# A mixture-of-experts stage: the seventeenth tile on the last place's weights, and gathers issued later

## The chip, the cores and the metric

The program runs on one core of a Trainium2 chip. The metric is the device time of one execution in microseconds (us), lower is better; of several runs the median counts. The engines are TensorE (PE, matrix products; its weight loads are shown as PEld), VectorE (DVE), ScalarE (ACT), GpSimd (POOL) and SyncE (SP), which here issues the plain DMAs. Gathers through a list of row numbers are issued by POOL. Each engine works through its instructions in the order in which the program gives them.

## The reference, cut to what matters

The reference computes four blocks of mixers on 512 tokens of width 1024, then a second network that ends with a mixture of experts. Only this last stage is touched. All of it is float32.

```python
def _moe(u, router_w, router_bias, w_gate, w_up, w_down):
    t = u.reshape(B * T, D)                              # 512 tokens x 1024
    s = jax.nn.sigmoid((t @ router_w).astype(jnp.float32))
    sb = s + router_bias.astype(jnp.float32)
    # the best of 4 groups of experts, and in it the best 2 of 4 experts
    ...
    combine = ...                                        # 512 x 16, two weights a token
    y = jnp.zeros_like(t)
    for e in range(16):
        h = jax.nn.silu(t @ w_gate[e]) * (t @ w_up[e])   # 1024 -> 512
        y = y + combine[:, e:e + 1] * (h @ w_down[e])    # 512 -> 1024
    return y
```

So each token uses two experts of 16, and how many tokens an expert gets is known only when the program runs: 1024 in all.

## The kernel before, in words

**Tiles.** The stage works on tiles of 128 tokens. Tiles 0 to 15 hold the first 128 tokens of experts 0 to 15. An expert with more tokens needs further tiles. The first of these is tile 16, which the program always computes; its expert's number is read at run time (`e0`, L3650). A loop behind the stage (`For_i`, L3696) would compute any others, one in each pass. `route` (L3374) works out on DVE and PE which tokens go where: `rsel` holds a token's rank among its expert's tokens, `rh` its number and its weight, `posf`/`pos` the row of its result, `ovl` the list of further tiles' experts and their count.

**A tile's work.** `own_hots` compares ranks with 1 to 128 (DVE), and `own` (through `metas`, L3550) multiplies the comparisons with `rh` on PE, which gives for each of the tile's 128 places the row number `ix` and the weight; then a gather (L3560, POOL) fetches these rows of `d_u` into `U[e]`. `turn_u` transposes them on PE and splits the result into a high part (ACT) and a low part (DVE). `up` multiplies with the gate weights (`pg`) and the up weights (`pu`), `gelu` combines the two, `turn_h` transposes again, `down` multiplies with the down weights, ACT scales the result (L3627), and `store` (L3630, SP) writes it to `d_o`. At the end the rows of `d_o` are gathered by `pos` (L3724) and added.

**Weights.** An expert has 12 units of 128 x 1024 numbers (512 KB): 4 gate, 4 up, 4 down. `moe_load` (L3505) issues their loads on SP, through 21 buffers. `split` (L3578) turns the next loaded unit into a high part, cast by ACT (L3582), and a low part, a subtraction (L3583) on POOL for every third unit (j % 3 == 2) and on DVE for the others. There are four buffers for split units. `mm3` (L169) multiplies high by high, high by low (L172 here waits for the weight's low part) and low by high.

**Order.** The order within the stage is written out by hand. For tile e the program goes through `up` for gate, `up` for up and then `down` of tile e - 1, unit by unit, with one `split` behind each unit's matmuls, three units ahead of their use. Of the twelve units that are split in a pass, numbered j modulo 12, gate has 11, 0, 1 and 2, up 3 to 6 and down 7 to 10; POOL's are 11, 2, 5 and 8. Other steps are put between: behind the second up unit (4) come `turn_u(e + 1)` and `own(e + 2)` with its gather, so that the gather stands on POOL ahead of the subtraction of unit 5. In this text "tile 8" as a stretch of time is the pass e = 8, with `down` of tile 7 in it.

Of the kernel before, what the change touches and what calls it, by code (L numbers as in the profile page):

```python
# [97 lines left out]
HLG = ()  # L98
HA = 2
NRAW = 13  # L100
RT_N = 288
NG = 4
PREP_US = 25.68
WG = 1
# [14 lines left out]
class Net:  # L119
# [2682 lines left out]
    def block2(self):  # L2802
        nc, A, v = self.nc, self.A, self.v
        V, S, G, MM = nc.vector, nc.scalar, nc.gpsimd, nc.tensor.matmul
# [486 lines left out]
        d_u = self.dram("d_u", [T, D])  # L3291
        self.raws = []
        units = []
        for e in range(16):
            units += [A["moe_w"][e, j] for j in range(8)] + ([A["moe_w"][e - 1, 8 + j] for j in range(4)] if e else [])
        self.mu = [units, ["wraw"] * 4 + ["whi"] * 2 + ["wlo"] * 2 + ["raw"] * NRAW, 0]
        for _ in range(4):
# [3 lines left out]
        U = {}  # L3301
# [26 lines left out]
        ps = self.psum()  # L3328
# [45 lines left out]
    def route(self, pool):  # L3374

        nc, A = self.nc, self.A
        V, S, G, MM = nc.vector, nc.scalar, nc.gpsimd, nc.tensor.matmul
        TTO = V.tensor_tensor
        lg = self.logits

        def t(name, *shape):
            return pool.tile([P] + list(shape), F32, name="r_" + name)
# [53 lines left out]
        M = []  # L3436
# [36 lines left out]
        V.tensor_copy(rh[:, :, :, 0], tok[:, :, None].to_broadcast([P, 4, 16]))  # L3473
        yield rsel, rh

        lst = t("lst", 8, 16)
        TTO(lst, ovb[:, None, :].to_broadcast([P, 8, 16]), co[:, 24:32, None].to_broadcast([P, 8, 16]), op=OP.is_le)
        oe = t("oe", 8)
        V.tensor_reduce(oe, lst, axis=AX.X, op=OP.add)
        V.tensor_scalar(oe, oe, -1.0, None, op0=OP.add)  # L3480
        V.tensor_reduce(oe[:, 7:8], ov, axis=AX.X, op=OP.add)
        ovl = rp.tile([P, 8], I32, name="ovl")
        V.tensor_copy(ovl, oe)

        r, ge = t("rk", 4, 16), t("ge", 4, 16)
        V.tensor_scalar(r, rsel, -1.0, None, op0=OP.add)
        V.tensor_scalar(ge, r, 127.5, None, op0=OP.is_ge)
        dl = t("dl", 16)
        TTO(dl, ovb, ce, op=OP.subtract)
        V.tensor_scalar(dl, dl, 15.0, 128.0, op0=OP.add, op1=OP.mult)  # L3490
        TTO(ge, ge, dl[:, None, :].to_broadcast([P, 4, 16]), op=OP.mult)
        TTO(r, r, ge, op=OP.add)
        V.scalar_tensor_tensor(r, ce[:, None, :].to_broadcast([P, 4, 16]), 128.0, r, op0=OP.mult, op1=OP.add)
        posf = rp.tile([P, 2, 4], F32, name="posf")
        for k in range(2):
            TTO(M[k], M[k], r, op=OP.mult)
# [3 lines left out]
        src = rp.tile([P, 2, 4, 2], F32, name="src")  # L3500
        V.tensor_copy(src[:, :, :, 0], tok[:, None, :].to_broadcast([P, 2, 4]))
        V.tensor_copy(src[:, :, :, 1], w)
        yield pos, posf, ovl, src

    def moe_load(self):  # L3505

# [15 lines left out]
    def moe(self):  # L3522
# [17 lines left out]
        M, U, UT, HT, TH, O = {}, {}, {}, {}, {}, {}  # L3540

        HOT = {}

# [6 lines left out]
        def metas(e, rhs):  # L3550

            pm = self.psum()
            for i, (o, r) in enumerate(zip(HOT.pop(e), rhs)):
                MM(pm[:, :2], o, r, start=(i == 0), stop=(i == len(rhs) - 1))
            m, ix = tl("meta", (P, 2), 4), tl("ix", (P, 1), 4, I32)
            V.tensor_copy(ix, pm[:, 0:1])
            V.tensor_copy(m, pm[:, 0:2])
            M[e] = m
            U[e] = tl("u", (P, D), 2)
            nc.gpsimd.indirect_dma_start(out=U[e], out_offset=None, in_=d_u,  # L3560
                                         in_offset=bass.IndirectOffsetOnAxis(ap=ix[:, 0:1], axis=0))

        def own_hots(e):
            hots(e, [rsel[:, a, e:e + 1] for a in range(4)], iota)
# [7 lines left out]
        def extra(e):  # L3572
            metas(e, [src[:, k, a, :] for k in range(2) for a in range(4)])
# [21 lines left out]
                self.split(o[:, 0, h:h + 4, :], o[:, 1, h:h + 4, :], p4)  # L3595
            return o

        def up(e, ps):

            for k2 in range(4):  # L3600
                w = W.pop(0)
                for kk in range(2):
                    k = 2 * k2 + kk
                    ws = slice(kk * 512, (kk + 1) * 512)
                    self.mm3(ps, UT[e][:, 0, k, :], UT[e][:, 1, k, :], w[:, 0, ws], w[:, 1, ws], k == 0, k == KC - 1)
# [10 lines left out]
        def down(e):  # L3616
            ps = [self.psum(), self.psum()]
            for k in range(4):
                w = W.pop(0)
                for n in range(2):  # L3620
                    ws = slice(n * 512, (n + 1) * 512)
                    self.mm3(ps[n], HT[e][:, 0, k, :], HT[e][:, 1, k, :], w[:, 0, ws], w[:, 1, ws], k == 0, k == 3)
                split()
                yield
            O[e] = tl("o", (P, D), 2)
            for n in range(2):
                S.activation(O[e][:, n * 512:(n + 1) * 512], ps[n], AF.Copy, scale=M[e][:, 1:2])  # L3627
# [12 lines left out]

        for e in range(2):
            own_hots(e)
            own(e)
        pos, posf, ovl, src = next(route)
# [5 lines left out]
        e0 = nc.values_load(ovl[0:1, 0:1], min_val=0, max_val=15, engines=(mybir.EngineType.SP,))  # L3650

        def unit(e, j):
            return A["moe_w"][bass.ds(e, 1), j].rearrange("o p c -> p (o c)")

        self.mu[0] += [unit(e0, j) for j in range(8)] + [A["moe_w"][15, 8 + j] for j in range(4)]
        self.mu[0] += [unit(e0, 8 + j) for j in range(4)]
        with self.tc.manual_schedule():
            for _ in range(3):
                split()
            turn_u(0)  # L3660
            for e in range(17):
                pg, pu = self.psum(), self.psum()
                for i, _ in enumerate(up(e, pg)):
                    if i == 0 and e:
                        turn_h(e - 1)
                    if i == 2:
                        if e < 14:
                            own_hots(e + 2)
                        elif e == 14:
                            extra_hots(16, base)  # L3670
                for i, _ in enumerate(up(e, pu)):
                    if i == 0 and e > 1:
                        store(e - 2, slot(e - 2))
                    if i == 1 and e < 16:
                        turn_u(e + 1)
                        if e < 14:
                            own(e + 2)
                        elif e == 14:
                            extra(16)
                for i, _ in enumerate(down(e - 1) if e else ()):  # L3680
                    if i == 0:
                        gelu(e, pg, pu)
                if not e:
                    gelu(e, pg, pu)
            turn_h(16)
            store(15, slot(15))
            for _ in down(16):
                pass
            store(16, slot(16))

        g2, lng, lnb = (self.wp.tile([P, UW], F32, name=n, tag="wraw", bufs=4) for n in ("g2", "lng", "lnb"))
        self.row_bcast(g2, self.mods["a4"][:, 40:48, 0])
        nc.sync.dma_start(lng, A["b2_l2g"].partition_broadcast(P))
        nc.sync.dma_start(lnb, A["b2_l2b"].partition_broadcast(P))
        n_ov = nc.values_load(ovl[0:1, 7:8], min_val=0, max_val=7)
        with self.tc.For_i(1, n_ov, 1) as i:  # L3696
            e = nc.values_load(ovl[0:1, bass.ds(i, 1)], min_val=0, max_val=15, engines=(mybir.EngineType.SP,))
# [6 lines left out]
            extra(17)  # L3704
            turn_u(17)
            for _ in range(4):
                split()
            pg, pu = self.psum(), self.psum()
            for ps in (pg, pu):
                for _ in up(17, ps):  # L3710
# [5 lines left out]
            store(17, d_o[bass.ds((i + 16) * P, P), :])  # L3716
        mst.close()

        tst, tp = self.open("tail")
# [74 lines left out]
def host_arrays(I):  # L3794
# [115 lines left out]
    co[:, 32:288] = (np.arange(16)[None] < np.arange(16)[:, None]).reshape(-1)  # L3910
# [27 lines left out]
```

## Time and profile before

| | |
|---|---|
| median of 3 runs | 3840.93 us (3830.1 to 3840.94) |
| the profiled execution | 3836.11 us, its span 3834.3 us |
| PE, DVE, ACT, POOL busy over the span | 87%, 65%, 45%, 35% |
| experts' stage, first matmul to last | 388.13 us, from 3388.87 to 3777.00 |
| loads of expert weights | 204 of 512 KB, 5.2 us from issue to landing |

The page of the profile shows the span in 40 slices of 96 us. The experts' stage fills the last slices but one: the row of DMA shares reads 8 (tenths) there, and the row of TensorE's granted clock, in tenths of 2.4 GHz, 9 in three slices. Groups of instructions by line, waits by line, single tiles and the timeline are asked of the trace separately; times in them are in us from the start of the span.

### The profile page before, as it was taken

What the parts mean: (1) busy time and instruction counts of PE and PEld (TensorE: products, weight loads), DVE (VectorE), ACT (ScalarE), POOL (GpSimd) and SP (SyncE); (2) the same over time, 40 slices, a digit from 0 to 9 for tenths busy, and PEclk for the clock granted to TensorE, in tenths of its full rate; (3) what the DMA queues carried; (4) which work ended last, traced back from release to release, by engine and by line L of the source; (5) the groups of instructions that cost most, each with busy time, mean ns of one, the idle gap of its engine ahead of it and who ended that gap; (6) DMA issues with size and microseconds to landing.
All of it is one profiled execution on the core that took longest, in us unless ns stands there. A gap on an engine that the chain in (4) does not pass through costs nothing. (4 is left out here: it accounts for less than half of the span.)

```text
span 3834.3 us, 63098 instructions
## 1 busy us (share of the span) xinstructions
PE 3337.1 (87%) x24502; PEld 2819.6 (74%) x24502; DVE 2500.9 (65%) x4375; ACT 1713.9 (45%) x2887; POOL 1327.4 (35%) x1559
## 2 busy tenths in 40 slices
PE   4999998988688889989989999899998785778883
PEld 3788887767577787777878887777886675667773
DVE  8777777453576767645445555556666789777767
ACT  4321223433455545645356666532223543346663
POOL 5031002220356767710043332202101556235555
PEclk8999998999788888899999999999998997779997
DMA  5444452246865344463422222345642210288883
GB/s 195 151 146 137 143 198 97 77 162 189 249 181 152 118 142 131 123 216 119 125 73 68 56 67 65 103 151 200 221 148 68 72 55 17 81 297 313 314 310 115
DMA packets 350861, 560.23 MB, mean 146 GB/s; under 512 B 170592, under 2 KB 226016, under 8 KB 350560
## 3 DMA queue, kind: packets, MB, share of 16 engines
q1 hardware_dynamic: 346960, 543.06, 43.7%
q0 software_dynamic: 3600, 13.11, 0.9%
q8 instruction: 194, 3.18, 0.3%
q14 instruction: 107, 0.88, 0.1%
HBM read 457.23 MB, written 88.36 MB: 142 GB/s over the span
## 5 line engine op out<-in xcount | busy, mean ns | idle before, releaser
L162 DVE TENSOR_TENSOR wlo<-wraw,whi 128x1024 fp32r<-128x1024 f32 x220 | 285.8, 1299 | 167.8 <-ACT whi L161 164.5
L171 PE MATMUL ps<-hl,whi 128*128 128x512 f32 (+1 forms) x992 | 363.9, 367 | 1.6 <-ACT hl L1945 1.6
L161 ACT CAST whi<-wraw 128x1024 fp32r<-128x1024 f32 x221 | 231.3, 1047 | 296.6 <-PE ps L172 183.1
L172 PE MATMUL ps<-hl,whi 128*128 128x512 f32 (+1 forms) x992 | 361.3, 364 | 1.5 <-DVE hl L1950 1.5
L173 PE MATMUL ps<-hl,wlo 128*128 128x512 f32 (+1 forms) x992 | 360.4, 363 | 2.5 <-DVE wlo L162 2.5
L3582 ACT CAST e_wsp<-mraw 128x1024 fp32r<-128x1024 f32 x204 | 212.4, 1050 | 105.0 <-issue 52.4
L3583 DVE TENSOR_TENSOR e_wsp<-mraw,e_wsp 128x1024 fp32r<-128x1024 f32 x136 | 187.2, 1399 | 72.9 <-ACT e_wsp L3582 71.6
L3583 POOL TENSOR_TENSOR e_wsp<-mraw,e_wsp 128x1024 fp32r<-128x1024 f32 x68 | 179.8, 2652 | 129.8 <-ACT e_wsp L3582 47.9
L173 PEld LDWEIGHTS ps<-hl,wlo 128*128 128x128 f32 x992 | 188.0, 189 | 34.5 <-DVE wlo L162 3.4
L172 PEld LDWEIGHTS ps<-hl,whi 128*128 128x128 f32 x992 | 187.8, 189 | 34.7 <-DVE hl L1950 4.9
L171 PEld LDWEIGHTS ps<-hl,whi 128*128 128x128 f32 x992 | 187.8, 189 | 32.1 <-ACT hl L1945 2.0
L1522 POOL TENSOR_TENSOR s_tmp<-s_N,s_P 128x15 f32<-128x15 f32 (+4 forms) x360 | 126.4, 351 | 145.4 <-DVE s_N L1506 119.0
L207 DVE SCALAR_TENSOR_TENSOR araw<-araw,conds 128x1024 f32<-128x1024 f32 x128 | 157.6, 1236 | 24.7 <-DMA araw<-ada 24.1
L171 PE MATMUL ps<-whi,hl 128*128 128x512 f32 x320 | 132.5, 414 | 27.3 <-ACT hl L404 25.6
L617 POOL TENSOR_SCALAR v<-v,vr_y 128x256 f32<-128x256 f32 x70 | 93.6, 1355 | 157.8 <-DVE vr_y L270 157.8
L171 PE MATMUL ps<-s,whi 128*128 128x512 f32 (+1 forms) x384 | 138.6, 361 | 0.0
L1523 POOL TENSOR_TENSOR s_P<-s_P,s_tmp 128x15 f32<-128x15 f32 (+4 forms) x360 | 127.5, 354 | 28.2
L172 PE MATMUL ps<-s,whi 128*128 128x512 f32 (+1 forms) x384 | 136.7, 356 | 0.0
L173 PE MATMUL ps<-s,wlo 128*128 128x512 f32 (+1 forms) x384 | 136.5, 356 | 0.2 <-DVE wlo L162 0.2
L172 PE MATMUL ps<-wlo,hl 128*128 128x512 f32 x320 | 132.6, 414 | 4.1 <-DVE wlo L162 3.9
L167 DVE TENSOR_TENSOR a_pt<-ps,a_pt 128x512 fp32r<-128x512 f32 (+1 forms) x128 | 69.3, 554 | 102.2 <-ACT a_pt L166 102.2
L173 PE MATMUL ps<-whi,hl 128*128 128x512 f32 x320 | 131.9, 412 | 1.4 <-DVE hl L411 1.3
(932 smaller groups left out, 10203.7 us busy)
## 6 DMA issues: line engine op xcount, KB each, us to landing
mraw<-moe_w SPq DMA_DIRECT2D x204, 512.0 KB, 5.2
araw<-ada SPq DMA_DIRECT2D x144, 512.0 KB, 3.9
wraw<-sgu_v SPq DMA_DIRECT2D x40, 512.0 KB, 3.6
wraw<-rw_in SPq DMA_DIRECT2D x40, 512.0 KB, 4.8
d_n<-ff SPq DMA_DIRECT2D x48, 384.0 KB, 5.2
s_fn<-d_n SPq DMA_DIRECT2D x24, 768.0 KB, 6.2
wraw<-sgu_out SPq DMA_DIRECT2D x34, 512.0 KB, 4.1
wraw<-sgu_u SPq DMA_DIRECT2D x32, 512.0 KB, 4.6
```

What stands on the lines that cost most here:

```text
L161: self.nc.scalar.copy(hi[:, :cols], t[:, :cols])
L162: (eng or self.nc.vector).tensor_tensor(lo[:, :cols], t[:, :cols], hi[:, :cols], op=OP.subtract)
L167: (eng or self.nc.vector).tensor_tensor(lo, src, hi, op=OP.subtract)
L171: mm(out, lh, rh, start=start, stop=False)
L172: mm(out, lh, rl, start=False, stop=False)
L173: mm(out, ll, rh, start=False, stop=stop)
L207: self.nc.vector.scalar_tensor_tensor(junk, w, 0.5, c, op0=OP.mult, op1=OP.mult, accum_out=out)
L617: e.tensor_scalar(vt[g][:, t, :], vt[g][:, t, :], r[:, t:t + 1], None, op0=OP.mult)
L1522: TTG(o, N[:, None, ts, s].to_broadcast([P, nj, nt]), Pm[:, js, s:s + 1].to_broadcast([P, nj, nt]), op=OP.mult)
L1523: TTG(Pm[:, js, ts], Pm[:, js, ts], o, op=OP.subtract)
L3582: S.copy(hl[:, 0, :], raw)
L3583: (G if j % 3 == 2 else V).tensor_tensor(hl[:, 1, :], raw, hl[:, 0, :], op=OP.subtract)
```

## The change

Experts and tiles are no longer the same numbers. A place (0 to 15) takes the part of the expert's number: the last expert that has more than 128 tokens, if it is not one of the first three (`MFIX`), changes places with expert 15. Tile 16 then belongs to the same expert as tile 15, and the two share each weight unit: `up` and `down` take several tiles, and a pass over tiles 15 and 16 multiplies both with a unit before the next. With that 192 units are loaded and split in place of 204. Where the last such expert is one of the first three, the loop behind the stage starts one tile earlier and computes tile 16 again with that expert's weights (`back`, `es[:, 1:2]`).

Weights of places 3 to 15 are now loaded from an address that SP reads from `ovl` (`placed`). `route` gets the operations that find the expert, exchange the two columns in `rsel` and `rh`, and write the list `il`. The table `low` is turned round (experts behind, not in front).

The gather is taken out of `metas` and becomes a step of its own. For tiles 0 to 2 and for tile 16 it stays where it was in POOL's order. For tiles 3 to 15 it is issued in `down` of the pass, behind the split of the second unit (8). `turn_u(16)` moves from the pass of tile 15 to the end of that of tile 14.

```diff
-RT_N = 288
+RT_N = 304
+MFIX = 3
+MOE_L = 33
@@ block2
-        for e in range(16):
+        for e in range(MFIX):
             units += [A["moe_w"][e, j] for j in range(8)] + ([A["moe_w"][e - 1, 8 + j] for j in range(4)] if e else [])
@@ route
-        lst = t("lst", 8, 16)
-        TTO(lst, ovb[:, None, :].to_broadcast([P, 8, 16]), co[:, 24:32, None].to_broadcast([P, 8, 16]), op=OP.is_le)
-        oe = t("oe", 8)
...
+        rs0 = t("rs0", 4, 16)
+        V.tensor_copy(rs0, rsel)
+        il = t("il", MOE_L)
+        es, no = t("es", 2), t("no", 16)
+        V.tensor_scalar(no, ovb, 0.5, None, op0=OP.is_ge)
+        V.tensor_reduce(es[:, 0:1], no, axis=AX.X, op=OP.add)
+        V.tensor_scalar(es[:, 1:2], es[:, 0:1], MFIX - 0.5, None, op0=OP.is_le)
+        oh, pe = t("oh", 16), il[:, 0:16]
+        V.memset(oh, 0.0)
+        V.tensor_scalar(oh[:, MFIX:], ce[:, MFIX:], es[:, 0:1], None, op0=OP.is_equal)
+
+        TTO(no, co[:, 288:304], oh, op=OP.mult)
+        TTO(pe, ce, no, op=OP.add)
+        V.tensor_reduce(es[:, 0:1], no, axis=AX.X, op=OP.add)
+        TTO(il[:, 15:16], il[:, 15:16], es[:, 0:1], op=OP.subtract)
+        for x in (rsel, rh[:, :, :, 1]):
+            d, ds_ = t("sw", 4, 16), t("sws", 4)
+            TTO(d, x[:, :, 15:16].to_broadcast([P, 4, 16]), x, op=OP.subtract)
+            TTO(d, d, oh[:, None, :].to_broadcast([P, 4, 16]), op=OP.mult)
+            TTO(x, x, d, op=OP.add)
+            V.tensor_reduce(ds_, d, axis=AX.X, op=OP.add)
+            TTO(x[:, :, 15], x[:, :, 15], ds_, op=OP.subtract)
+
+        xi = t("xi", 8)
...
+        ovl = rp.tile([P, MOE_L], I32, name="ovl")
+        V.tensor_copy(ovl, il)
+        back = rp.tile([P, 1], F32, name="back")
+        V.tensor_scalar(back, es[:, 1:2], float(P), None, op0=OP.mult)
@@ metas
-            M[e] = m
+            M[e], IX[e] = m, ix
+
+        def gather(e):
             U[e] = tl("u", (P, D), 2)
...
@@ up, down
-        def up(e, ps):
+        def up(*tiles):
             for k2 in range(4):
                 w = W.pop(0)
-                for kk in range(2):
...
+                for e, ps in tiles:
+                    for kk in range(2):
+                        k = 2 * k2 + kk
+                        ws = slice(kk * 512, (kk + 1) * 512)
+                        self.mm3(ps, UT[e][:, 0, k, :], UT[e][:, 1, k, :], w[:, 0, ws], w[:, 1, ws], k == 0, k == KC - 1)
                 split()
                 yield
@@ the stage
-        self.mu[0] += [unit(e0, j) for j in range(8)] + [A["moe_w"][15, 8 + j] for j in range(4)]
-        self.mu[0] += [unit(e0, 8 + j) for j in range(4)]
+        at = {}
+        def placed(e, j):
+            if e not in at:
+                at[e] = nc.values_load(ovl[0:1, e:e + 1], min_val=MFIX, max_val=15, engines=(mybir.EngineType.SP,))
+            return unit(at[e], j)
+        for e in range(MFIX, 17):
+            self.mu[0] += [lambda e=e, j=j: placed(e, j) for j in range(8 if e < 16 else 0)]
+            self.mu[0] += [A["moe_w"][e - 1, 8 + j] if e == MFIX else lambda e=e, j=j: placed(e - 1, 8 + j) for j in range(4)]
...
-            for e in range(17):
-                pg, pu = self.psum(), self.psum()
-                for i, _ in enumerate(up(e, pg)):
+            for e in range(16):
+                own_e = (e, 16) if e == 15 else (e,)
+                pg, pu = ({t: self.psum() for t in own_e} for _ in range(2))
+                for i, _ in enumerate(up(*pg.items())):
...
-                    if i == 1 and e < 16:
+                    if i == 1 and e < 15:
                         turn_u(e + 1)
                         if e < 14:
                             own(e + 2)
                         elif e == 14:
                             extra(16)
+                            gather(16)
                 for i, _ in enumerate(down(e - 1) if e else ()):
                     if i == 0:
-                        gelu(e, pg, pu)
+                        for t in own_e:
+                            gelu(t, pg[t], pu[t])
+                    if i == 1 and e < 14:
+                        gather(e + 2)
+                    if i == 3 and e == 14:
+                        turn_u(16)
                 if not e:
-                    gelu(e, pg, pu)
-            turn_h(16)
-            store(15, slot(15))
-            for _ in down(16):
+                    gelu(e, pg[e], pu[e])
+                    gather(2)
+            for t in (15, 16):
+                turn_h(t)
+            store(14, slot(14))
+            for _ in down(15, 16):
                 pass
-            store(16, slot(16))
+            for t in (15, 16):
+                store(t, slot(t))
```

## Rows read from the trace of the kernel before

**Rows 1.** Windows: stretch, length; engines' busy us; granted clock, DMA share, GB/s.

```profile
3388.87:3777.00 388.13, 343.04 (x1549) 277.99 (x1549) 283.71 (x313) 258.51 (x301) 203.57 (x82) 0.94 0.84 291
3584.95:3606.92 21.97, 18.94 (x92) 15.55 (x93) 16.50 (x19) 15.38 (x18) 12.23 (x6) 1.00 0.94 343
3606.92:3630.45 23.53, 20.52 (x92) 16.69 (x92) 16.48 (x19) 15.39 (x18) 12.16 (x6) 0.93 0.90 299
3491.00:3494.40 3.40, 3.40 (x9) 2.65 (x9) 0.12 (x1) 1.04 (x1) 2.06 (x1) 0.50 1.03 400
3367.00:3381.00 14.00, 7.05 (x33) 6.97 (x33) 8.52 (x41) 0.17 (x1) 0.46 (x1) 0.50 0.98 393
```

**Rows 2.** The tile mraw: loads, casts, and us from issue to landing.

```profile
L3519 SPq DMA_DIRECT2D mraw<-moe_w x204: 327/328/629, 3281.8 to 3740.0; - x102
...
L3582 ACT CAST e_wsp<-mraw x204: 1027/1052/1069, 3362.0 to 3768.4; 128x1024 fp32r<-128x1024 f32 x102
...
DMA to landing us min/median/max: 3.2/5.2/10.2
```

**Rows 3.** Waits in the stage: total us, times, longest.

```profile
PE ps L172 <- POOL e_wsp L3583: 40.5, 14, 3.0
```

**Rows 4.** Timeline of tile 8: start, us, engine, line, names, [idle before].

```profile
3576.55 0.95 PE L3554 MATMUL ps<-rh,e_hot 128*128 128x2 f32 x8
...
3577.27 1.06 ACT L3582 CAST e_wsp<-mraw 128x1024 fp32r<-128x1024 f32 x1
...
3580.15 2.54 DVE L3583 TENSOR_TENSOR e_wsp<-mraw,e_wsp 128x1024 fp32r<-128x1024 f32 x2
...
3580.34 1.87 POOL L3560 DMA_INDIRECT e_u<-d_u,e_ix  x1 [4.48 <-DVE e_meta L3557]
...
3582.23 5.03 POOL L3583 TENSOR_TENSOR e_wsp<-mraw,e_wsp 128x1024 fp32r<-128x1024 f32 x2
...
3584.95 0.50 PE L172 MATMUL ps<-e_wsp,e_hT 128*128 128x512 f32 x1 [3.02 <-POOL e_wsp L3583]
```

**Rows 5.** Timeline of PE: ends of the waits in tiles 2 and 14.

```profile
3444.21 0.79 PE L172 MATMUL ps<-e_wsp,e_hT 128*128 128x512 f32 x1 [3.03 <-POOL e_wsp L3583]
...
3725.52 0.50 PE L172 MATMUL ps<-e_wsp,e_hT 128*128 128x512 f32 x1 [3.03 <-POOL e_wsp L3583]
```

**Rows 6.** Timeline of PE and POOL in tile 15 and behind it.

```profile
3731.10 0.39 PE L171 MATMUL ps<-e_wsp,e_uT 128*128 128x512 f32 x1
...
3739.76 0.49 PE L3593 MATMUL ps<-ident,e_u 128*128 128x128 f32 x3
...
3746.19 3.26 POOL L3583 TENSOR_TENSOR e_wsp<-mraw,e_wsp 128x1024 fp32r<-128x1024 f32 x1 [1.23 <-issue]
...
3749.03 0.39 PE L171 MATMUL ps<-e_wsp,e_uT 128*128 128x512 f32 x1
...
3751.15 2.80 POOL L3583 TENSOR_TENSOR e_wsp<-mraw,e_wsp 128x1024 fp32r<-128x1024 f32 x1 [1.70 <-ACT e_wsp L3582]
```

**Rows 7.** The tile e_u (gathers): durations, first and last start; us to landing.

```profile
L3560 POOL DMA_INDIRECT e_u<-d_u,e_ix x15: 958/1760/1960, 3401.8 to 3720.8; - x15
...
DMA to landing us min/median/max: 4.9/8.2/8.7
```

**Rows 8.** Timeline of DVE where the stage begins.

```profile
3386.03 0.17 DVE L3499 CAST pos<-posf 128x8 int32<-128x8 f32 x1
...
3388.85 0.69 DVE L167 TENSOR_TENSOR e_uT<-ps,e_uT 128x512 fp32r<-128x512 f32 x1 [2.65 <-ACT e_uT L166]
```

**Rows 9.** The tile e_o (stores): us from issue to landing, shortest, median, longest.

```profile
DMA to landing us min/median/max: 2.6/6.6/7.0
```

**Rows 10.** Timeline of DVE, POOL and PE in tile 1.

```profile
3417.56 7.37 DVE L3583 TENSOR_TENSOR e_wsp<-mraw,e_wsp 128x1024 fp32r<-128x1024 f32 x2 [0.64 <-ACT e_wsp L3582]
...
3418.11 5.73 POOL L3583 TENSOR_TENSOR e_wsp<-mraw,e_wsp 128x1024 fp32r<-128x1024 f32 x2
...
3424.98 0.50 PE L172 MATMUL ps<-e_wsp,e_hT 128*128 128x512 f32 x1 [1.40 <-DVE e_wsp L3583]
```

More of the change, by code (lines that the diff above doesn't have):

```diff
@@ L3474, in route @@
         yield rsel, rh
-        lst = t("lst", 8, 16)
-        TTO(lst, ovb[:, None, :].to_broadcast([P, 8, 16]), co[:, 24:32, None].to_broadcast([P, 8, 16]), op=OP.is_le)
-        oe = t("oe", 8)
[L3479 to L3483, printed above, removed]
+        rs0 = t("rs0", 4, 16)
+        V.tensor_copy(rs0, rsel)
@@ new lines, in route @@
+        xi = t("xi", 8)
+        V.tensor_scalar(xi, co[:, 24:32], es[:, 1:2], None, op0=OP.subtract)
+        lst = m16[:, :8]
+        TTO(lst, ovb[:, None, :].to_broadcast([P, 8, 16]), xi[:, :, None].to_broadcast([P, 8, 16]), op=OP.is_gt)
+        V.tensor_reduce(il[:, 16:24], lst, axis=AX.X, op=OP.add)
+        V.tensor_scalar(il[:, 16:24], il[:, 16:24], 15.0, None, op0=OP.min)
+        V.tensor_scalar(il[:, 24:32], xi, 16.0, None, op0=OP.add)
+        V.tensor_reduce(il[:, 32:33], ov, axis=AX.X, op=OP.add)
@@ L3485, in route @@
+        TTO(il[:, 32:33], il[:, 32:33], es[:, 1:2], op=OP.add)
+        ovl = rp.tile([P, MOE_L], I32, name="ovl")
+        V.tensor_copy(ovl, il)
+        back = rp.tile([P, 1], F32, name="back")
+        V.tensor_scalar(back, es[:, 1:2], float(P), None, op0=OP.mult)
         r, ge = t("rk", 4, 16), t("ge", 4, 16)
-        V.tensor_scalar(r, rsel, -1.0, None, op0=OP.add)
+        V.tensor_scalar(r, rs0, -1.0, None, op0=OP.add)
         V.tensor_scalar(ge, r, 127.5, None, op0=OP.is_ge)
         dl = t("dl", 16)
-        TTO(dl, ovb, ce, op=OP.subtract)
+        TTO(dl, ovb, pe, op=OP.subtract)
@@ L3492, in route @@
         TTO(r, r, ge, op=OP.add)
-        V.scalar_tensor_tensor(r, ce[:, None, :].to_broadcast([P, 4, 16]), 128.0, r, op0=OP.mult, op1=OP.add)
+        V.scalar_tensor_tensor(r, pe[:, None, :].to_broadcast([P, 4, 16]), 128.0, r, op0=OP.mult, op1=OP.add)
         posf = rp.tile([P, 2, 4], F32, name="posf")
@@ L3502, in route @@
         V.tensor_copy(src[:, :, :, 1], w)
-        yield pos, posf, ovl, src
+        yield pos, posf, ovl, src, back
     def moe_load(self):
@@ L3539, in moe @@
         nc.sync.dma_start(iota, A["rt_iota"])
-        M, U, UT, HT, TH, O = {}, {}, {}, {}, {}, {}
+        M, IX, U, UT, HT, TH, O = {}, {}, {}, {}, {}, {}, {}
         HOT = {}
@@ L3557, in metas @@
             V.tensor_copy(m, pm[:, 0:2])
-            M[e] = m
+            M[e], IX[e] = m, ix
+        def gather(e):
             U[e] = tl("u", (P, D), 2)
             nc.gpsimd.indirect_dma_start(out=U[e], out_offset=None, in_=d_u,
-                                         in_offset=bass.IndirectOffsetOnAxis(ap=ix[:, 0:1], axis=0))
+                                         in_offset=bass.IndirectOffsetOnAxis(ap=IX.pop(e)[:, 0:1], axis=0))
         def own_hots(e):
@@ L3596, in turned @@
             return o
-        def up(e, ps):
+        def up(*tiles):
             for k2 in range(4):
                 w = W.pop(0)
-                for kk in range(2):
-                    k = 2 * k2 + kk
-                    ws = slice(kk * 512, (kk + 1) * 512)
-                    self.mm3(ps, UT[e][:, 0, k, :], UT[e][:, 1, k, :], w[:, 0, ws], w[:, 1, ws], k == 0, k == KC - 1)
+                for e, ps in tiles:
[3 more added lines that the diff above has]
+                        self.mm3(ps, UT[e][:, 0, k, :], UT[e][:, 1, k, :], w[:, 0, ws], w[:, 1, ws], k == 0, k == KC - 1)
                 split()
@@ L3614, in gelu, with down @@
             TH[e] = t
-        def down(e):
-            ps = [self.psum(), self.psum()]
+        def down(*tiles):
+            ps = {e: [self.psum(), self.psum()] for e in tiles}
             for k in range(4):
                 w = W.pop(0)
-                for n in range(2):
-                    ws = slice(n * 512, (n + 1) * 512)
-                    self.mm3(ps[n], HT[e][:, 0, k, :], HT[e][:, 1, k, :], w[:, 0, ws], w[:, 1, ws], k == 0, k == 3)
+                for e in tiles:
+                    for n in range(2):
+                        ws = slice(n * 512, (n + 1) * 512)
+                        self.mm3(ps[e][n], HT[e][:, 0, k, :], HT[e][:, 1, k, :], w[:, 0, ws], w[:, 1, ws], k == 0, k == 3)
                 split()
                 yield
-            O[e] = tl("o", (P, D), 2)
-            for n in range(2):
-                S.activation(O[e][:, n * 512:(n + 1) * 512], ps[n], AF.Copy, scale=M[e][:, 1:2])
+            for e in tiles:
+                O[e] = tl("o", (P, D), 2)
+                for n in range(2):
+                    S.activation(O[e][:, n * 512:(n + 1) * 512], ps[e][n], AF.Copy, scale=M[e][:, 1:2])
         def store(e, dst):
@@ L3643, in moe @@
             own(e)
-        pos, posf, ovl, src = next(route)
+            gather(e)
+        pos, posf, ovl, src, back = next(route)
         rst.close()
@@ L3649, in moe @@
         V.tensor_scalar(base, iota, 16.0 * P - 1, None, op0=OP.add)
-        e0 = nc.values_load(ovl[0:1, 0:1], min_val=0, max_val=15, engines=(mybir.EngineType.SP,))
         def unit(e, j):
             return A["moe_w"][bass.ds(e, 1), j].rearrange("o p c -> p (o c)")
-        self.mu[0] += [unit(e0, j) for j in range(8)] + [A["moe_w"][15, 8 + j] for j in range(4)]
-        self.mu[0] += [unit(e0, 8 + j) for j in range(4)]
+        at = {}
[6 more added lines that the diff above has]
+            self.mu[0] += [A["moe_w"][e - 1, 8 + j] if e == MFIX else lambda e=e, j=j: placed(e - 1, 8 + j) for j in range(4)]
         with self.tc.manual_schedule():
@@ L3670, in moe @@
                             extra_hots(16, base)
-                for i, _ in enumerate(up(e, pu)):
+                for i, _ in enumerate(up(*pu.items())):
                     if i == 0 and e > 1:
                         store(e - 2, slot(e - 2))
-                    if i == 1 and e < 16:
+                    if i == 1 and e < 15:
                         turn_u(e + 1)
@@ L3694, in moe @@
         nc.sync.dma_start(lnb, A["b2_l2b"].partition_broadcast(P))
-        n_ov = nc.values_load(ovl[0:1, 7:8], min_val=0, max_val=7)
+        V.tensor_scalar(base, base, back, None, op0=OP.subtract)
+        n_ov = nc.values_load(ovl[0:1, 32:33], min_val=0, max_val=8)
         with self.tc.For_i(1, n_ov, 1) as i:
-            e = nc.values_load(ovl[0:1, bass.ds(i, 1)], min_val=0, max_val=15, engines=(mybir.EngineType.SP,))
+            e, at = (nc.values_load(ovl[0:1, bass.ds(i + o, 1)], min_val=m, max_val=m + n, engines=(mybir.EngineType.SP,))
+                     for o, m, n in ((16, 0, 15), (24, 16, 6)))
             V.tensor_scalar(base, base, float(P), None, op0=OP.add)
@@ L3704, in moe @@
             extra(17)
+            gather(17)
             turn_u(17)
@@ L3709, in moe @@
             for ps in (pg, pu):
-                for _ in up(17, ps):
+                for _ in up((17, ps)):
                     pass
@@ L3715, in moe @@
                 pass
-            store(17, d_o[bass.ds((i + 16) * P, P), :])
+            store(17, d_o[bass.ds(at * P, P), :])
         mst.close()
@@ L3909, in host_arrays @@
     co[:, 24:32] = np.arange(8)
-    co[:, 32:288] = (np.arange(16)[None] < np.arange(16)[:, None]).reshape(-1)
+    co[:, 32:288] = (np.arange(16)[None] > np.arange(16)[:, None]).reshape(-1)
+    co[:, 288:304] = 15 - np.arange(16)
     A["rt_const"] = co
```

## The prediction

> **What bounds the kernel now.** The experts' stage takes 388 us, and busy times by window come first [rows 1]: TensorE (PE) is busy for 343 of them, VectorE (DVE) for 284, ScalarE for 259, POOL for 204, and the DMA engines have a share of 0.84. None is full. The share asks first whether the stage waits for its weights. It doesn't: the answer for the tile mraw [rows 2] has the last of the 204 loads issued at 3740.0 us and its cast started at 3768.4; with the median landing of 5.2 us it lay ready for 23 us. What the stage loses is in the list of waits [rows 3]: PE stands idle before L172, the product with a weight's low half, for 40.5 us in 14 times, longest 3.0, each until POOL has written e_wsp.
>
> The timeline shows why [rows 4]. At 3577.27 ScalarE casts unit 101 and is done at 3578.33; its low half is POOL's. But POOL's next instruction in its own order is the gather (L3560), which waits for its row numbers until 3580.34 and then takes 1.87 us. Only at 3582.23 does the subtraction start, the first of two merged in that row, and PE, which has run out of halves, resumes at 3584.95 after 3.02 us. Without the gather the half would have been there near 3580.9 (half of the 5.03 behind 3578.33), before PE asks at 3581.93.
>
> The price is more than the wait. From the end of one such wait to the end of another it is 281.31 us for 12 tiles, 3444.21 to 3725.52 [rows 5], 23.44 each; 21.97 in the tile where the granted clock stays at 1.00 (2.4 GHz), 23.53 in one with a mean of 0.93 [rows 1]. A stretch that begins where such a wait ends has 0.50 (1.2 GHz). 281.31 less 12 x 21.97 and 0.95 (a second lookup in tile 14) leaves 16.7, so ten or eleven of the twelve paid the clock's 1.56. Without wait and lower clock a tile takes 21.97 - 3.02 = 18.95 us. A second way to that number: tile 15, behind which no gather stands, needs 3749.03 - 3731.10 = 17.93 us [rows 6]; with the eight small matmuls of 0.95 that look up a tile's rows [rows 4] it is 18.88.
>
> **The change, part by part.** *The later gather.* Tiles 1 to 13 issue it four units further on, behind gelu and behind the second of POOL's two subtractions there. The row numbers have long been ready at that point, so POOL neither waits nor holds up these two halves. Gone are 1.18 us in tile 1 (40.5 less 13 x 3.025), 3.03 in tile 2, and wait and clock in tiles 3 to 13; the wait of tile 14 stays, since gather(16) is still issued at once. The gather's own time, 1.76 at the median [rows 7], falls between POOL's units 8 and 11 of the twelve. In tile 15 the first of these ends at 3749.45, 0.42 us after the next tile's first matmul, and the next starts 1.70 us later at 3751.15 [rows 6]: the gather just fits. gather(2) keeps its place between the same two subtractions.
>
> What is late next is the gather itself. It moves some 5 us towards its reader, the transposes of turn_u. These start 3739.76 - 3731.10 = 8.66 us into a tile [rows 6]; the gather starts at 0.42, so its rows have 8.24 us to land. Gathers land after 4.9 to 8.7 us, median 8.2 [rows 7]. PE's wait at turn_u is therefore between nothing and 0.46 by these rows. I take 0.4 per tile, near the long end, because a faster stage leaves the DMA engines less idle. A tile is then 19.35 us.
>
> *The shared weights.* PE has as many matmuls as before: tile 16's move next to tile 15's. Gone are 12 loads, 12 casts and 12 subtractions. None of the 14 waits lies behind 3725.52 [rows 5], so in the last tiles they are hidden behind matmuls, and I take nothing for them; in the joint stretch each unit serves twice the matmuls, and the cover only grows. turn_u(16) moves to the end of tile 14, at 3731.10 by today's times; its gather starts at 3720.8 [rows 7] and has 10.3 us, more than 8.7. Zero, and 0.5 either way.
>
> *Loads with an address from a register*, 156 more, and a register load for each of 13 tiles: on SP alone, ahead by the 23 us above. Zero; 1 us a tile on SP would stay hidden as well.
>
> *The route's new instructions.* Some 24 more small DVE operations stand ahead of the stage, each about 0.1 to 0.2 us like the one of 0.17 at 3386.03 [rows 8]: 2.4 to 4.8 us. DVE idles 2.65 us there before the first tile's low half [rows 8]. So 0 to 2.2 us late; I take 1.
>
> *The end.* Two stores, of tiles 15 and 16, leave together in place of one. A store lands after 2.6 us at the least, 6.6 at the median, beside loads, and 7.0 at most [rows 9]. So 0 to 4.4 more; I take 2, half way, since only one other store runs beside it. The output scalings follow their banks one by one, as they do now.
>
> **The sum**, against the profiled execution's 3836.11 us. The 12 tiles after the change: 12 x 19.35 = 232.2, and tile 14's wait of 3.03 and second lookup of 0.95, together 236.2; saved 281.3 - 236.2 = 45.1. With 3.03 and 1.18 from tiles 2 and 1 it is 49.3; less 1 and 2 at the two ends 46.3. The time is 3790 us. The median of the runs, 3840.93, lies 4.8 above the profiled execution, the fastest, 3830.1, 6 below; the range takes that in.
>
> **Rivals.** *The DMA engines become the bound, through the gather.* Shares of two tiles [rows 1] make 0.94 x 21.97 = 20.7 and 0.90 x 23.53 = 21.2 us of DMA work. At 19.35 a tile the weights fall behind by 1.3 to 1.9 us each time, up to 22 over 12 tiles, which the lead of 23 just covers; the gather has no lead, and waits for the backlog. A tile then takes about 20.9 us, 12 of them and 3.98 make 254.8, and the time is 3836.1 - 26.5 - 4.2 + 3 = 3808. For it: 343 and 299 GB/s at shares of 0.94 and 0.90. Against it: loads alone reached 393 GB/s [rows 1], so a packet's time in the share is partly waiting. Chance 0.22.
>
> *The subtraction moved forward collides with DVE's.* In tile 1 two subtractions of POOL took 5.73 us beside two of DVE that took 7.37 [rows 10] in place of 2.54 [rows 4], and PE then waited 1.40 us for DVE. If each tile gets that wait, it is 20.75 us a tile, 253 with the 3.98, and tile 1 gains nothing: 3836.1 - 28.3 - 3.0 + 3 = 3808. The Trainium skill, GPSIMD Engine Reference, Specifications, says that GpSimd's SBUF interface is shared with VectorE and contended by instructions with two SBUF inputs, as DVE's subtraction is. By that rule this rival would be the forecast; the trace agrees in rows 10. Against it: in tile 15 the same subtractions ran without a gather between, and no wait for DVE came [rows 6]; in tile 1 POOL's two ran back to back. Chance 0.08.
>
> *No small cost comes*: 18.88 us a tile, nothing at either end: 281.3 - 230.5 + 4.2 = 55, so 3781 us. Chance 0.07.
>
> *The gather lands far too late, and the kernel is slower.* Place: turn_u, 13 times. Beyond a landing of 8.24 us each microsecond costs 13, and waits of 3 us brought 1.56 us of lower clock with them in most tiles. The gains of 51 (without the 0.4) are gone at a wait of about 2.8, a landing near 11; at 12.5 it is 13 x (4.3 + 1.56) = 76, and the time 3861. For it: loads have taken up to 10.2 us to land [rows 2]. Against it: no gather took over 8.7 while loads and stores ran, and a slower PE lets a backlog clear. The Trainium skill, DMA: Bandwidth & Descriptors, Queues, rings and completion order, says that a DMA engine takes turns between queues packet by packet; by it a gather, on its own queue, doesn't stand behind the whole backlog, which this rival needs. Chance 0.04.
>
> *The change doesn't do what it says here*: were the last expert with more than 128 tokens one of the first three, the loop behind the stage would run once, some 36 us (a tile of 18.9 and unhidden landings of 5.2, 8.2 and 3.6), so 3826. The reference on its inputs sends 159 tokens to expert 6 and at most 117 to any other, and 204 loads are 17 tiles of 12 [rows 2]. Chance 0.03.
>
> **How the numbers follow.** The forecast's own case (18.9 to 20 us a tile, 3781 to 3798) has 0.56. A change under 0.3%, about 11.5 us, can't be told from none here. The forecast, the two rivals near 3808 and the full gain are faster by more: 0.93; the loop falls within it: 0.03; slower 0.04. The range for 8 in 10 runs from 3776 (full gain, and a fast run) to 3814 (the rivals near 3808, and the runs' spread).
>
> **What would show it.** Right: PE's waits before L172 until POOL drop from 14 to one or two, the granted clock is 1.00 through tiles 3 to 13, tiles take 19 to 20 us, and POOL's gather stands directly behind a subtraction. PE's only new waits are under 1 us before turn_u's transposes, until e_u has landed. Wrong: waits of over 1 us there (the DMA rival), waits until DVE's e_wsp (the collision), or a stage that starts more than 2 us later.

## The result, and the profile after

The changed kernel takes 3782.68 us (median of 4 runs, 3772.47 to 3786.45) against 3835.91 before (4 runs on the same chip): a ratio of 0.9858, 95% interval 0.9834 to 0.9882. A second set of 5 gave 3786.09, ratio 0.9875 (0.9854 to 0.9896). The forecast was 3790, the range 3776 to 3814.

The profiled execution (3786.45 us, span 3784.7) is 49.6 us shorter than the one before. Three marks part this: the first matmul that looks up rows, the stage's first and last product (starts), and the span's end. What lies ahead of the first mark has the same code and was 5.3 us longer; it varies from run to run. From that mark on:

| us | start | stage | end | sum |
|---|---|---|---|---|
| before | 8.76 | 387.91 | 57.55 | 454.2 |
| after | 9.41 | 328.73 | 61.09 | 399.2 |

So 55.0 us are gone: 59.2 in the stage, with 4.2 given back at its two ends. This sum is used below wherever few us matter, since the first mark itself lay between 3372.9 and 3390.8 us in fourteen profiles.

Windows of the changed kernel (columns as in [rows 1]): the stage, the twelve tiles from turn_u(3) to turn_u(15), one of them, and the stretch behind the one wait that is left.

```profile
3394.84:3723.57 328.73, 321.54 (x1548) 265.61 (x1548) 282.78 (x312) 245.46 (x289) 191.66 (x78) 0.99 0.83 317
3437.47:3664.56 227.09, 225.38 (x1105) 186.71 (x1105) 215.32 (x229) 184.86 (x216) 148.51 (x61) 1.00 1.01 389
3551.55:3570.22 18.67, 18.67 (x92) 15.69 (x93) 17.00 (x17) 15.40 (x18) 11.69 (x5) 1.00 1.01 395
3673.80:3680.60 6.80, 5.87 (x14) 4.61 (x15) 2.78 (x3) 1.82 (x2) 3.21 (x2) 0.50 0.10 39
```

The twelve tiles took 280.4 us before and take 227.1: 18.92 each. PE is busy for 225.38 of these, at a granted clock of 1.00. PE's waits from the first look-up on (us in total, times, longest; L174 is the old L172):

```profile
PE ps L3626 <- DMA e_u<-d_u,e_ix: 5.7, 5, 4.1
PE ps L174 <- POOL e_wsp L3616: 3.0, 1, 3.0
```

Of 14 waits for POOL's low half [rows 3] one is left, in tile 14, whose gather(16) still follows its look-up at once. Behind it the clock is 0.50, as it was in [rows 1]. Of the five waits for e_u the one of 4.1 is the first tile's; the other four are 0.22 to 0.67. Tile 8 in the timeline:

```profile
3555.12 0.14 DVE L3587 CAST e_ix<-ps 128x1 int32<-128x1 f32 x1
...
3558.94 2.41 POOL L3616 TENSOR_TENSOR e_wsp<-mraw,e_wsp 128x1024 fp32r<-128x1024 f32 x1 [2.14 <-issue]
...
3560.25 3.31 DVE L3616 TENSOR_TENSOR e_wsp<-mraw,e_wsp 128x1024 fp32r<-128x1024 f32 x2
...
3561.49 1.76 POOL L3593 DMA_INDIRECT e_u<-d_u,e_ix  x1
...
3563.68 2.41 POOL L3616 TENSOR_TENSOR e_wsp<-mraw,e_wsp 128x1024 fp32r<-128x1024 f32 x1 [0.43 <-ACT e_wsp L3615]
...
3570.22 1.04 PE L3626 MATMUL ps<-ident,e_u 128*128 128x128 f32 x8
```

Where [rows 4] had POOL idle for 4.48 us ahead of the gather, it now stands directly behind a subtraction, 6.2 us after its row numbers were written, and ends 0.43 us before POOL's next operands are there. It takes longer to land than in [rows 7], and turn_u starts 0.04 or 0.05 us after the landing in 9 of 13 tiles:

```profile
L3593 POOL DMA_INDIRECT e_u<-d_u,e_ix x17: 946/1764/1837, 3387.8 to 3670.1; - x17
...
DMA to landing us min/median/max: 4.9/8.6/9.3
```

The end, SP and POOL. Here the two stores are followed on SP by the row loads lng and lnb (rows of the last normalization); the second landed 6.4 us after its issue, at 3732.03, and the gathers of y start behind it, 9.83 us after the last product (6.14 before):

```profile
3723.35 1.69 SPq L3666 DMA_DIRECT2D d_eo<-e_o  x2
...
3725.14 0.42 SPq L3748 DMA_DIRECT2D lng<-b_l2g  x1
3725.64 0.73 SPq L3749 DMA_DIRECT2D lnb<-b_l2b  x1
3733.40 0.96 POOL L3782 DMA_INDIRECT y<-d_eo,pos  x1 [17.83 <-issue]
```

Before, lnb stood behind the last store as well, and landed 5.6 us after its issue, near 3785.1. But SP had passed the entry of the loop behind the stage (L3696) ahead of both, and the gathers of y started before lnb had landed. First the step at the entry, then SP and POOL:

```profile
3778.93 0.04 SPq L3696
```

```profile
3779.09 0.33 SPq L3630 DMA_DIRECT2D d_eo<-e_o  x1
3779.48 1.66 SPq L3694 DMA_DIRECT2D lnb<-b_l2b  x1
3782.92 0.96 POOL L3724 DMA_INDIRECT y<-d_eo,pos  x1 [10.95 <-DMA d_eo<-e_o]
```

In the changed kernel that entry (L3752) lies behind all four transfers. The chain that ended last goes through it from 3732.13, 0.10 us behind lnb's landing, to POOL's last step there:

```profile
3732.52 0.03 POOLq L3752
```

### The profile page after: what moved, and what is told of

The parts are those of the page before. It is cut to its first block, busy times and chain, and to the rows that moved or that the text cites. A ratio compares the mean times of both kernels' runs of the same rounds, so it can differ in the third digit from the quotient of the medians.

```text
span 3784.7 us, 63370 instructions
## 1 busy us (share of the span) xinstructions
PE 3309.5 (87%) x24502; PEld 2799.8 (74%) x24502; DVE 2501.4 (66%) x4392; ACT 1700.2 (45%) x2875; POOL 1310.9 (35%) x1555
## 5 line engine op out<-in xcount | busy, mean ns | idle before, releaser
L174 PE MATMUL ps<-hl,whi 128*128 128x512 f32 (+1 forms) x992 | 360.9, 364 | 2.0 <-DVE hl L1952 2.0
L3615 ACT CAST e_wsp<-mraw 128x1024 fp32r<-128x1024 f32 x192 | 200.2, 1052 | 55.5 <-PE ps L175 34.1
L3616 POOL TENSOR_TENSOR e_wsp<-mraw,e_wsp 128x1024 fp32r<-128x1024 f32 x64 | 167.5, 2618 | 136.1 <-ACT e_wsp L3615 68.8
L174 PEld LDWEIGHTS ps<-hl,whi 128*128 128x128 f32 x992 | 187.8, 189 | 34.2 <-DVE hl L1952 4.1
L174 PE MATMUL ps<-s,whi 128*128 128x512 f32 (+1 forms) x384 | 136.8, 356 | 0.0
L174 PE MATMUL ps<-wlo,hl 128*128 128x512 f32 x320 | 132.8, 415 | 2.9 <-DVE wlo L164 2.7
```

The source lines that it names most:

```text
L174: mm(out, lh, rl, start=False, stop=False)
L3615: S.copy(hl[:, 0, :], raw)
L3616: (G if j % 3 == 2 else V).tensor_tensor(hl[:, 1, :], raw, hl[:, 0, :], op=OP.subtract)
```

## The experiments

"Before" is the kernel before, on the same chip. The sums are start + stage + end as above.

**Which part brings the gain.** The first run is the kernel before with the later gather alone, the second the changed kernel with the gather put back.

```diff
# e1: kernel before
+                    if i == 1 and e < 14:
+                        gather(e + 2)        # in down, no longer in metas
# e2: changed kernel
                             own(e + 2)
+                            gather(e + 2)    # at the old place
...
-                    if i == 1 and e < 14:
-                        gather(e + 2)
```

> The kernel before with the later gather of tiles 3 to 15 alone, weights not shared. Theory (the gather is the whole gain; it stopped POOL, whose subtraction PE waited for): the stage gets some 57 us shorter, as after the change up to tile 14 (53.3 in tiles 3 to 14, 3.2 in tile 1, 0.3 before), and the time lies 57 us under before, a ratio near 0.985, tiles 3 to 14 at 18.9 us, DMA share near 1.0 in them. Rival (sharing carries a part, through the 12 loads and splits that it saves): at most 45 us under before.

> The changed kernel with every gather issued at once behind its lookup, as before; weights shared. Theory (sharing saves nothing on the path): 13 waits of 3.0 us for POOL stay, with the lower clock behind most; the stage's last part is 2.4 us shorter, its start 0.7 and its end 3.7 us later: +2 us, within 6 of before. Rival (sharing is worth its 12 loads and splits): 5 us or more under before.

e1: 3781.98 us, ratio 0.985 (0.9826 to 0.9874), sum 397.3. e2: 3836.07, ratio 0.9999 (0.9984 to 1.0013), sum 451.3. PE's waits for POOL in e1, then e2:

```profile
PE ps L172 <- POOL e_wsp L3585: 0.9, 1, 0.9
```

```profile
PE ps L174 <- POOL e_wsp L3616: 40.5, 14, 3.0
```

All 14 waits stand in e2 as in [rows 3]. The later gather is the whole gain; the shared weights bring none that can be measured. In e1, tile 14 has the collision that the prediction gave as a rival: there PE's wait of 0.9 us for POOL is followed by one of 1.4 for DVE, whose two subtractions take 7.11 us beside POOL's, as in [rows 10].

**Is it the wait for row numbers, or the gather's own time on POOL?** Here the gather stays ahead of unit 5 but the look-up is done one pass earlier, so that its row numbers are there (tile 16's too). e4 does the same in the changed kernel.

```diff
# e3: kernel before; e4: changed kernel
-                            own_hots(e + 2)
+                            own_hots(e + 3)
...
+                        gather(e + 2)        # its row numbers are a pass old
-                            own(e + 2)
+                            own(e + 3)
```

> The kernel before, its gathers at their old place ahead of POOL's unit 5, but the lookups of row numbers one pass earlier (own(e+3) and tile 16's in place of own(e+2)), so that a gather finds its rows' numbers there. Theory (POOL was held up by the wait for row numbers, not by the gather's own 1.8 us, for which POOL idled 4.5 us): no wait of PE for POOL is left, in tile 14 neither; 57 us and some 5 more for tile 14, 62 under before; the gather lands some 5 us before its reader. Rival (the gather's own time on POOL counts): PE waits 1 us or more per tile for POOL's halves, and the gain is 45 us or less.

> The changed kernel (weights shared) with the gathers back at their old place and the lookups one pass earlier, tile 16's too. Theory: against the change it gains tile 14's wait and its clock, some 5 us, and the 0.1 us a tile by which the gather's landing gates turn_u: 6 us under the change, 59 under before. Rival (the DMA engines, at a share of 1.01, set the 18.9 us a tile, and the gather's landing only shows it): tiles stay at 18.9 us and PE waits somewhere else for a transfer.

e3: 3774.61 us, ratio 0.9839 (0.9817 to 0.9861), sum 389.5. e4: 3770.78, ratio 0.983 (0.9807 to 0.9852), sum 392.7. PE waits for POOL nowhere in e3's stage, with the gather at its old place. Its landings:

```profile
L3562 POOL DMA_INDIRECT e_u<-d_u,e_ix x17: 953/961/1767, 3379.6 to 3654.4; - x17
...
DMA to landing us min/median/max: 4.6/8.1/8.9
```

The wait for row numbers held POOL, not the gather's 1 to 1.8 us. With some 10 us between landing and turn_u, e3's tiles 2 to 13 take 18.63 to 18.73 us, against 18.92 in the changed kernel: the gather's late landing costs 0.25 a tile. In e9, the same kernel again, a tile takes 18.83, and the cost is 0.16. The DMA engines, at a share of 1.01, do not set the 18.92: at the same share e4's tiles take 18.65 to 18.73 too.

**What lengthens the end.** The loads of lng and lnb go ahead of the joint down, in the changed kernel (e5) and in e4 (e6).

```diff
+            nc.sync.dma_start(lng, ...)
+            nc.sync.dma_start(lnb, ...)
             for _ in down(15, 16):
```

> The changed kernel, with one edit: the loads of the two rows lng and lnb are issued before the joint down of tiles 15 and 16 (that is, ahead of the stores of these tiles on SP) and not behind them. In the changed kernel's trace the first gather of y starts 9.8 us after the stage's last matmul, against 6.1 before the change. Theory A: this extra time is that of the two row loads, which now stand behind the stores, and whose landing the loop's entry waits for; then the gather of y starts 5.7 to 6.5 us after the last matmul and the time falls by 3 to 4 us, to about 3779. Theory B (the prediction's): it is the second store that leaves together with the first; then the gather of y stays at 9 to 10 us and the time does not change.

> The changed kernel with two edits: the look-up of a tile's rows is done one pass earlier, so that its gather can be issued at its old place without a wait, and the loads of lng and lnb are issued ahead of the joint down of tiles 15 and 16. If the two savings add (12 us from the earlier look-up by the run that had it, 3.7 from the row loads), the time is about 3767, ratio 0.982, with the gather of y about 6 us after the last matmul. If the end is set by the second store (rival), it is 3771, as without the second edit.

e5: 3781.11 us, ratio 0.985 (0.9815 to 0.9886), sum 394.9. e6: 3771.6, ratio 0.9826 (0.9806 to 0.9845), sum 388.9. SP and POOL at the end of e5:

```profile
3715.52 1.35 SPq L3742 DMA_DIRECT2D lng<-b_l2g  x1
3716.98 0.47 SPq L3743 DMA_DIRECT2D lnb<-b_l2b  x1
3727.29 1.70 SPq L3666 DMA_DIRECT2D d_eo<-e_o  x2
```

```profile
3733.36 0.96 POOL L3782 DMA_INDIRECT y<-d_eo,pos  x1 [13.86 <-issue]
```

The gather of y now starts 5.85 us after the last product (5.86 in e6), and the end is 57.0: the row loads were the 4 us, and the two stores cost nothing against before (57.55). The medians don't show it: e5 was expected at about 3779 and e6 at 3767, and e6 lies no lower than e4. The 4 us are smaller than what precedes the stage moves by (e5's runs span 3770.6 to 3795.1).

**How near the DMA engines are to being the bound.** The changed kernel with added loads in passes 2 to 14 into a buffer that nothing reads: 512 KB a pass (e7), 896 KB (e8).

```diff
+                    if i == 0 and 2 <= e < 15:          # e8: i % 2 == 0, 896 columns
+                        nc.sync.dma_start(xp.tile([P, 1024], F32, name="more", bufs=1), A["moe_w"][0, i][:, :1024])
```

> The changed kernel, with one added load of 512 KB in each of the passes 2 to 14 on SP, into a buffer that nothing reads. It asks how far the DMA engines are from being the bound. In the changed kernel they move 389 GB/s, with a share of 1.01, and a tile takes 18.92 us. Theory A (DMA engines have nothing left at this rate): each tile needs 1.35 us more of them; the lead of the weights' loads shrinks from about 22 us by 1.35 a tile to about 5, the gathers land later than 9.3 us, and PE waits at turn_u by 1 us or more in the last tiles; the time is up by 5 to 18 us. Theory B (the engines still have room): the lead stays at about 20 us, the traffic goes to 416 GB/s, and the time stays within 3 us of the changed kernel's.

> As the run with one more load, but with two of 448 KB in each of the passes 2 to 14, 2.36 us more of the DMA engines for each tile at 389 GB/s. Theory A (nothing left): 13 x 2.36 = 30.7 us of loads fall behind, more than the lead of 22; PE waits for weights in the last tiles, and the time is up by 9 to 30 us. Theory B (room left): the traffic goes to 437 GB/s, the lead stays, and the time is up by at most 5 us. In between (a top rate of 400 to 420 GB/s) the lead shrinks by 1 to 1.7 us a tile without reaching zero.

e7: 3772.89 us, ratio 0.9834 (0.9814 to 0.9854), sum 396.5. e8: 3780.89, ratio 0.9852 (0.9831 to 0.9873), sum 396.4. The twelve tiles, of e7 and of e8:

```profile
3425.19:3650.65 225.46, 224.73 (x1105) 186.69 (x1105) 215.57 (x229) 184.86 (x216) 150.62 (x61) 1.00 1.02 414
```

```profile
3436.00:3661.26 225.26, 224.58 (x1104) 186.68 (x1105) 215.60 (x229) 184.89 (x216) 150.50 (x61) 1.00 1.03 413
```

e7 went as theory B had it: 414 GB/s, and the issues kept their lead, though the loads' lead shrank: one had landed 25 us before its cast at 3437.7 us, another 20 us before the one at 3644.4. Its sum is 2.7 below the changed kernel's: 1.6 in the twelve tiles, which move by 1.1 between two runs of the changed kernel (227.1 and 226.0 in e9), and 1.2 behind them, where the lower clock behind tile 14's wait lasted 3.4 us and not 6.8. e8 is the case in between: 437 GB/s would have been needed, the engines gave 413, and the weights fell behind. A load had landed 25 us before its cast at 3448.5 us and 9 us before the one at 3655.1, yet the tiles got no longer. By these two runs the top is near 414 GB/s, at a share of 1.02 to 1.03. A tile moves 12 units, a gather and a store, 14 x 0.524 = 7.3 MB, which is 17.7 us at that rate, a microsecond below PE's 18.7. In e8 the weights' landing went from a median of 6.6 us in the changed kernel to 10.0; that of the gathers did not grow (8.6 there). First the weights', then the gathers', in e8:

```profile
DMA to landing us min/median/max: 3.4/10.0/11.8
```

```profile
DMA to landing us min/median/max: 5.2/8.2/9.0
```

The Trainium skill, DMA: Bandwidth & Descriptors, Queues, rings and completion order, says that an engine takes turns between queues; by it a gather doesn't stand behind the backlog of SP's loads, and these two rows agree.

**Together, on one chip.**

> The changed kernel as it is, beside the two that follow, on one chip, because what comes before the experts' stage moves by several microseconds from run to run (the stage's first matmul came between 3382 and 3400 us in nine profiles, with the same code ahead of it). By its stage (58 to 60 us shorter), its start (0.7 longer) and its end (3.6 longer) it should be 55 us below the kernel before, ratio 0.9857. By the prediction's sum it would be 46, ratio 0.988.

> The changed kernel with rows looked up one pass earlier and the loads of lng and lnb issued ahead of the joint down. By the profiles its stage is 6.9 us shorter than the changed kernel's (321.8 against 328.7) and its end 4.0 shorter (57.1 against 61.1), its start 0.6 longer: 10 us, or 0.27%, below it.

> The kernel before with only the earlier look-up: no shared weights, no register addresses, gathers at their old place. Its stage is 323.3 us, its start 8.9 and its end 57.3 in the profile. If sharing weights is worth nothing even where no wait is left, it lies within 1.5 us of the run with both. Rival: with the waits gone the last two tiles' weights become the limit and sharing brings 3 us or more.

| | median us | ratio | sum us |
|---|---|---|---|
| e9, changed kernel | 3786.09 | 0.9875 (0.9854 to 0.9896) | 398.9 |
| e10, as e6 | 3775.05 | 0.9849 (0.9827 to 0.9871) | 388.8 |
| e11, as e3 | 3768.89 | 0.984 (0.9817 to 0.9864) | 389.0 |

Both are below the changed kernel, by 10 us in the sums; the intervals of the ratios alone overlap with its. The kernel before with the early look-up alone (e11) is as fast as the one with shared weights too. In e10 sharing makes the stage 1.6 us shorter and the start 1.5 longer. But PE still waits there in tile 14's pass, 0.3 us for POOL and 1.4 for DVE, and behind it 0.4 for the low part of turn_u(16), none of which e11 has; what sharing brings without these waits no run shows.

**What lengthens the start.** In the nine profiles with shared weights so far it is 9.2 to 10.5 us, in the four without 8.5 to 8.9. The last run is e6 with one line more:

```diff
+        placed(MFIX, 0)       # reads the first address where the kernel before read e0
         for e in range(MFIX, 17):
```

> The run with the earlier look-up and the earlier row loads, and one line more: SP reads its first address from ovl before the three splits ahead of the first pass, as the kernel before did with e0, so that the three loads behind that read wait until route has written ovl. In the runs with shared weights 24 weight loads are issued before the first gather, the last of which land 2.8 to 5.0 us behind its start; it lands after 5.0 to 6.3 us, and the stage starts 9.2 to 10.5 us after the first look-up. Without shared weights it is 21 loads, all landed by then, a landing of 4.4 to 4.6 us and a start of 8.5 to 8.9. Theory A (the three loads beside it slow the first gather): 21 loads, a landing of 4.4 to 4.7, a start of 8.5 to 9.0. Theory B (the prediction's: the route's added DVE operations delay the start): the start stays at 9.2 us or more. The time moves by at most 1.5 us, less than the runs can tell.

3772.21 us, ratio 0.9838 (0.9818 to 0.9857), sum 388.1. In the kernel before SP stood 13.6 us at the read of e0, and three loads behind it:

```profile
SPq L3650 <- DVE r_rk L3493: 13.6, 1, 13.6
```

In the changed kernel they go out at once, the last lands 3.2 us after the first gather's start, and the stage begins when that gather has landed (5.2 us; 4.6 before). PE there, in the changed kernel and in e12:

```profile
3393.05 1.97 PE L3626 MATMUL ps<-ident,e_u 128*128 128x128 f32 x8 [4.07 <-DMA e_u<-d_u,e_ix]
```

```profile
3389.22 1.94 PE L3626 MATMUL ps<-ident,e_u 128*128 128x128 f32 x8 [1.60 <-DMA e_u<-d_u,e_ix]
```

With the loads held again the landing is 4.4 us and the start 8.61: theory A. The route's added operations, all still there, cost nothing.

## Why the prediction was right, and where it was not

*The wait and the clock: right.* 14 waits became one, the granted clock was 1.00 for 276.5 us on end, and the gather stands directly behind a subtraction. e1 and e2 show that this is the whole gain, and e3 that the row numbers were what POOL waited for.

*A tile without a wait: mis-sized, 18.67 and not 18.95.* The prediction took the shown 3.02 us of idle time off 21.97. The price of a wait is more. Here is PE ahead of the wait of [rows 4] and behind it:

```profile
3581.32 0.39 PE L173 MATMUL ps<-e_wsp,e_hT 128*128 128x512 f32 x1
3581.54 0.39 PE L171 MATMUL ps<-e_wsp,e_hT 128*128 128x512 f32 x1
...
3585.29 0.40 PE L173 MATMUL ps<-e_wsp,e_hT 128*128 128x512 f32 x1
```

Matmuls start 0.225 us apart though each lasts 0.39. Over the wait the starts are 3.41 apart (3584.95 - 3581.54), the next 0.34: 3.75 for two steps of 0.225, a loss of 3.30. And 21.97 - 3.30 = 18.67, the length of tile 8 in the changed kernel above. The 280.4 us before are then 12 x 18.67, 12 x 3.30, and 16.8 of lower clock (what the tiles had above 21.97). The prediction's second way, 17.93 and 0.95 for the look-up, is 0.21 too long as well; I did not take that apart, and so that the two ways agreed proved nothing. The Trainium skill, TensorE: Matmul & The Clock Gate, Step-by-step: what each phase is for, says that the drain of a matmul lies over the next one; an idle time counted from its end leaves that out, and the rows agree.

*The late gather: right mechanism, 0.25 a tile (0.16 in e9) in place of 0.4.* With the last point a tile is 18.92 and not 19.35: 5.2 us over twelve.

*Tile 1: 3.15 us saved in place of 1.18.* Its wait for DVE [rows 10], 1.40, went too, since the gather no longer sets POOL's two subtractions beside DVE's two; with 0.28 more for each wait, 1.18 + 1.40 + 0.56 = 3.14.

*The shared weights: zero, right in total.* In the stage they save little: from the end of tile 14's wait to the last product it is 48.84 us and was 51.26, which I did not take apart, and e4's stage is 1.4 shorter than e3's. Start and end give back 4.2.

*The start (1 us; 0.65): right in size, by a wrong cause.* It is the first gather's landing beside three loads (e12), not the route.

*The end (2 us; 3.5): wrong cause.* The two stores cost nothing; the row loads behind them do, now that SP passes the loop's entry after them and waits there for their landing (e5). The prediction did not follow SP past the last store.

*The sum.* 46.3 was forecast and 55.0 came: 5.2 from the tiles, 2.0 from tile 1, 2.4 behind tile 14, 0.3 each from tile 0 and the start, less 1.5 at the end. Against the medians 53 us are gone in the first set. That is nearer to the rival without small costs (55) than to the forecast, though for other reasons: the small costs came, and the gain was larger. In the second set (e9) it is 47, the forecast's number; its interval holds 46 and 55 alike, and its sum, 398.9, says 55.

*The rivals.* The DMA engines did not become the bound: 20.7 to 21.2 us of work a tile was read from their share, and a share of 1.01 to 1.03 went with 389 to 414 GB/s; by bytes and the top rate of e7 and e8 it is 17.7. The collision did not come in the changed kernel: DVE's pairs take up to 3.3 us in tile 8, but PE does not wait for DVE. It came once in e1 and once in each of e4, e6, e10 and e12, for 1.4 us in tile 14. The gather landed after at most 9.3 us.

## What to carry to other kernels

A queue that stands still holds what is behind it: look for an instruction that waits in front of work whose operands are ready, and either move it back or, better, have its operand made earlier (e3 beats the later gather by 0.16 to 0.25 us a tile). Price a wait on TensorE from start to start, with the lower clock behind it, not by its idle time. When a change removes a stall on a DMA queue or adds a last transfer to it, follow what that queue issues next and who waits for its landing.

## What the runs showed of the hardware that was not expected

- A DMA share near 1 is not the limit: 389 GB/s and 414 GB/s were moved at 1.01 and 1.02, and [rows 1] had 343 at 0.94.
- Three weight loads of 512 KB in flight beside a gather of the same size made its landing 5.0 to 6.3 us in place of 4.4 to 4.6.
- Waits on PE of 3.02 us were followed by the lower clock in 10 of the twelve tiles; one of 1.4 us behind 0.3 (e6) was not: its clock stayed at 1.00 for 324 us.
